# A hybrid decoder layer on one core: full 128-row low parts of the keys in the attention scores

## The chip, the cores and the metric

The kernel runs on one core of one Trainium2 chip. The time is device microseconds of an execution, given as the median of several runs. A profile is one more execution, taken by the hardware profiler; its span reaches from the first to the last instruction. TensorE (PE) multiplies, with its weight loads shown apart (PEld); VectorE (DVE), ScalarE (ACT) and GpSimd (POOL) do the elementwise work; SyncE (SP) issues the DMAs.

## What is computed

One decoder layer for 512 tokens of width 1024 in fp32: a token mixer of three groups (sparse attention, gMLP, a Conformer convolution), cross-attention into 256 memory tokens, and a gated ConvFFN. The change lies in the sparse attention. It has 8 heads of width 64 in 2 key/value groups; with 512 tokens, all 8 blocks of the selected branch are taken and the window covers everything, so both branches are causal softmax attention, each with its own keys and values, beside a compressed branch:

```python
s_s = jnp.einsum("bgrtd,bgtmd->bgrtm", qb, gk).astype(jnp.float32) * scale
p_s = masked_softmax(s_s, mask_s)
o_s = jnp.einsum("bgrtm,bgtmd->bgrtd", p_s.astype(gv.dtype), gv)
...
s_w = jnp.einsum("bgrtd,bgkd->bgrtk", qb, kw).astype(jnp.float32) * scale
p_w = masked_softmax(s_w, mask_w)
o_w = jnp.einsum("bgrtk,bgkd->bgrtd", p_w.astype(vw.dtype), vw)
...
o = (gates[..., 0:1] * unblock(o_c) + gates[..., 1:2] * unblock(o_s)
     + gates[..., 2:3] * unblock(o_w))
```

## The kernel before

Every factor of a product is split into a high part that TensorE's faster fp32 form holds exactly and a low rest, so that a product takes three matmuls (high x high, high x low, low x high).

**Keys and queries.** Tokens lie along the free dimension, head dimensions along the 128 rows. `ev_q` (line 566) makes one 128-row tile per head, with the high part of the query in the 64 rows of its group g and the low part in the other 64. `ev_k` (line 584) makes for each branch b: for each group a tile `kh_[b, g]` with the high part of the keys in both halves, and one tile `kl_[b]` with the low parts, group 0 in rows 0 to 63 and group 1 in rows 64 to 127. All of these tiles are slabs, 56 buffers of 128 x 512 that are used in turn.

**Scores.** `scores()` (line 985) goes through 16 units (token block i of 128, group g, branch b), four heads in each, and W = 128 (i + 1) keys. A head takes a pair of matmuls into one bank, with the query tile as the weights. The first contracts all 128 rows and so gives (high + low query) x high key; the second contracts the 64 rows of the group and gives high query x low key:

```python
E.matmul(o3[:, jj, :], q, kh_[b, g][:, :W], start=True, stop=False)
E.matmul(o3[:, jj, :], q[hs], kl_[b][hs, :W], start=False, stop=True)
```

Four heads of 128 keys, two of 256, or one of 384 or 512 go into one bank (tag "s", two banks).

**What follows a score.** `soft` (line 1006): VectorE adds the mask and takes the row extreme, ScalarE takes the exponential with its sum, VectorE the reciprocal, GpSimd scales by reciprocal and gate (tiles "tpr"). `turns` and `mix`: TensorE transposes the probabilities, ScalarE and VectorE split them into high ("tB") and low ("tC"), and TensorE multiplies both with the values into one bank. Work on the compressed branch ("tcd", "tcph", "tcpl"), on the memory's keys and values (weights "whi" and "wlo", split by ScalarE and, for the memory, GpSimd), the gMLP and the convolution is mixed in.

**What sets the order.** Each engine executes its instructions in the order in which the program issues them. From line 452 on, that order is made while the program is built: `Lanes` (line 44) holds many generators, books an assumed cost for every instruction (line 65) and lets that step go next which can start first by these costs, by priority among near equals. A matmul's cost there goes by its columns. All instructions are issued through line 186, so the rows of the trace are told apart by their tiles.

Of the kernel before, what the change touches and what calls it, by code (L numbers as in the profile page):

```python
# [9 lines left out]
F32 = mybir.dt.float32  # L10
# [31 lines left out]


class Lanes:
    """Puts the steps of concurrent generators in order: each generator yields the engine of its next step, what the
    step reads and the kinds of slots it opens; the step that can start first goes next, and among those of one
    engine that are about as early, the most urgent one."""

    LAT = {"E": 0.18, "S": 0.14, "V": 0.12, "G": 0.14, "D": 0.0}
    OWN = {"E": 0.0, "S": 0.05, "V": 0.12, "G": 0.05, "D": 0.0}  # L50
# [139 lines left out]
def body(ctx, tc, xT, memT, memN, cmask, cmaskT, w_a, w_v, w_u, w_c1, gains, smalls, ws_t, bcs, w_o, w_q, w_k, w_vm,  # L190
# [3 lines left out]
    ln = Lanes(PB)  # L194
    V, S, G, E, Q = [Engine(ln, k, e) for k, e in zip("VSGED", (nc.vector, nc.scalar, nc.gpsimd, nc.tensor, nc.sync))]
# [11 lines left out]
    def nm(s):  # L207
        uid[0] += 1
        return f"{s}_{uid[0]}"

    def slab(shape=(P, T), dt=F32R):
        return psl.tile(list(shape), dt, name=nm("sl"), tag="slab", bufs=NSLAB)

    def tmp(tag, shape=(P, T), dt=F32):
        return ln.open(tag, pt.tile(list(shape), dt, name=nm("t" + tag), tag=tag, bufs=TB[tag]))

    def tiny(shape, dt=F32):
        return pt.tile(list(shape), dt, name=nm("ty"), tag="tiny", bufs=24)
# [4 lines left out]
    def col(n):  # L223
        return pt.tile([P, n], F32, name=nm("rc"), tag="rcol", bufs=4)

    def ps(tag):
        return ln.open(tag, pp.tile([P, T], F32, name=nm("ps"), tag="bank", bufs=8))
# [12 lines left out]
    def mm3(o, ah, al, bh, bl, start, stop):  # L240
        E.matmul(o, ah, bh, start=start, stop=False)
        E.matmul(o, ah, bl, start=False, stop=False)
        E.matmul(o, al, bh, start=False, stop=stop)
# [10 lines left out]
        for _ in gen:  # L254
            pass

    # weight stream
    specs = [(("a", m), w_a[m], (8, 128)) for m in range(12)]
    specs += [(("c1", i), w_c1[i], (16, 64)) for i in range(2)]
    specs += [(("v", c), w_v[:, k0:k1, :], (k1 - k0, 280)) for c, (k0, k1) in enumerate(((0, 3), (3, 6), (6, 8)))]  # L260
# [9 lines left out]
    order = {s[0]: n for n, s in enumerate(specs)}  # L270
# [32 lines left out]
    def ahead(key, n=2):  # L303
        prep(order[key] + n)

    # constants
    gn = pc.tile([P, NGAIN], F32, name="gn")
    sm = pc.tile([P, NSMALL], F32, name="sm")
    cm = pc.tile([P, T], F32, name="cm")
# [1 line left out]
    def gv(name):  # L311
        a, b = GAIN[name]
        return gn[:, a:b]
# [55 lines left out]
            mm3(o[:, :width], wh[:, k, :], wl[:, k, :], hi, lo, first and n == 0, last and n == len(ks) - 1)  # L369
            yield  # L370

    # start: first norm and the first two column tiles side by side
    n1 = Norm("g_mix")
    x = [slab(dt=F32) for _ in range(KD)]
    # wake the activation table and the tensor engine's clock while the first loads run
    wz = tmp("A")
    V.memset(wz, 0.0)
    S.activation(tiny([P, 4]), wz[:, 0:4], AF.Copy)
# [70 lines left out]
    wsr = slab(dt=F32)  # L449
    load(wsr, ws_t)  # L450

    # from here on lanes
    for tag, n in list(PB.items()) + list(TB.items()) + [("raw", NRAW), ("whi", NW), ("wlo", NW), ("bank", 8)]:
        ln.slots[tag] = [0.0] * n
    for o, tag in zip(zc, ("mm", "mm", "s", "s")):
# [14 lines left out]
    def pr(kind, j=0):  # L470
        return prio[kind][j]
# [32 lines left out]
    def spent(key):  # L504
        ln.done(*ready.pop(key))

    # depthwise convolution
    cw = pc.tile([P, 62], F32, name="cwh")
    V.tensor_scalar(cw, sv("cw"), 0.5, None, op0=ALU.mult)
    conv_acc = [slab(dt=F32) for _ in range(2)]  # L510
# [28 lines left out]
                                   op0=ALU.mult, op1=ALU.add)  # L539
        ln.mark(("taps", c), acc)  # L540

    # projection tiles
    qs, kh_, kl_ = {}, {}, {}

    def ev_cmp(kv, o):
# [38 lines left out]
    def ev_k(b, o):  # L584
        yield "V", [o], ["A"]
        kf = tmp("A")
        V.tensor_mul(kf, o, r_bc)
        ln.done(o)
        kl_[b] = slab()
        for g in range(2):  # L590
            kh_[b, g] = slab()
            hs = slice(64 * g, 64 * g + 64)
            for half in (g, 1 - g):
                yield "S", [kf], []
                S.activation(kh_[b, g][64 * half:64 * half + 64], kf[hs], AF.Copy)
            yield "V", [kh_[b, g]], []
            V.tensor_sub(kl_[b][hs], kf[hs], kh_[b, g][hs].bitcast(F32))
        ln.done(kf)
        ln.mark(("k", b), kl_[b], kh_[b, 0], kh_[b, 1])

    vs, gate, gz = [None] * NT, [None] * NT, [slab([P, 2, 256], F32) for _ in range(NT)]

# [82 lines left out]
                ln.add(pr("ev", 4), ev_u(hf, i, o))  # L685
        ln.mark("projected")

    # compressed blocks: second layer and scores of all tokens
    w2 = pc.tile([64, 2, 192], F32R, name="w2s")
    split(w2[:, 0, :], w2[:, 1, :], sv("w2")[0:64, :])  # L690
    vcz, kcz, sct = [], [], []
# [64 lines left out]
        for i in range(NT):  # L756
            ln.add(pr("cmp", i), compressed(i))

    # memory: statistics and parts, then keys and values as filler
    rm_col = col(2)  # L760
    rm_bc = pt.tile([P, MEM], F32, name="rm_bc", tag="rmbc", bufs=1)
    g_m = gv("g_m")
# [86 lines left out]
                ln.add(pr("memev", 1), mem_ev("mv", 2 * c + mt, o))  # L849
        ln.mark("quiet")  # L850

    # token-major tails of the gMLP and convolution groups
    g_out = gv("g_out")
    y_hi, y_lo = [None] * KD, [None] * KD
    gx = []
# [121 lines left out]
        yield from put_back(y, 6, i)  # L977
        ln.done(y)

    # native sparse attention  # L980
    units = [(i, g, b) for i in range(NT) for g in range(2) for b in range(2)]
    probs, left = {}, {}
    cmp_p, yts = {}, {}
# [1 line left out]
    def scores():  # L985
        yield "E", ["attend"], []
        for u in units:
            i, g, b = u
            W = P * (i + 1)
            hp = {0: 4, 1: 2, 2: 1, 3: 1}[i]  # L990
            hs = slice(64 * g, 64 * g + 64)
            isl = slice(i * P, (i + 1) * P)
            probs[u], left[u] = [None] * 4, 4
            mn, sm_ = tiny([P, 4]), tiny([P, 4])
            for n in range(4 // hp):
                yield "E", [("q", 4 * g + n * hp + jj) for jj in range(hp)] + [("k", b)], ["s", "pr"], pr("score", i)
                o = ps("s")
                p_ = tmp("pr")
                o3 = o[:, :hp * W].rearrange("p (h w) -> p h w", h=hp)
                for jj in range(hp):  # L1000
                    q = qs[4 * g + n * hp + jj][:, isl]
                    E.matmul(o3[:, jj, :], q, kh_[b, g][:, :W], start=True, stop=False)
                    E.matmul(o3[:, jj, :], q[hs], kl_[b][hs, :W], start=False, stop=True)
                ln.add(pr("soft", i), soft(u, n * hp, hp, o, p_, mn, sm_))

    def soft(u, j0, hp, o, p_, mn, sm_):
        i, g, b = u
        W = P * (i + 1)
        o3 = o[:, :hp * W].rearrange("p (h w) -> p h w", h=hp)
        p3 = p_[:, :hp * W].rearrange("p (h w) -> p h w", h=hp)  # L1010
        for jj in range(hp):
            yield "V", [o], []
            V.tensor_tensor_reduce(out=p3[:, jj, :], in0=o3[:, jj, :], in1=cm[:, T - W:], scale=1.0, scalar=3e38,
                                   op0=ALU.add, op1=ALU.min, accum_out=mn[:, j0 + jj:j0 + jj + 1])
        ln.done(o)
        for jj in range(hp):
            yield "S", [p_], []
            S.activation(p3[:, jj, :], p3[:, jj, :], AF.Exp, scale=-1.0, bias=mn[:, j0 + jj:j0 + jj + 1],
                         accum_out=sm_[:, j0 + jj:j0 + jj + 1])
        yield "V", [p_, ("v", i)], []  # L1020
        f = tiny([P, hp])
        V.reciprocal(f, sm_[:, j0:j0 + hp])
        for jj in range(hp):
            yield "G", [f, p_], []
            G.tensor_scalar(p3[:, jj, :], p3[:, jj, :], f[:, jj:jj + 1],
                            gate[i][:, 4 * g + j0 + jj, 1 + b:2 + b], op0=ALU.mult, op1=ALU.mult)
            probs[u][j0 + jj] = p3[:, jj, :]
        left[u] -= hp
        if left[u] == 0:
            ln.mark(("p", u), *probs[u])  # L1030
# [140 lines left out]
                                   y_hi[kt][:, isl].bitcast(F32), op0=ALU.mult, op1=ALU.subtract)  # L1171
        ln.mark(("yn", i), *y_lo[:4])

    # projections of the residual stream
    def tiles(name, parts, deps, after, phases):
        """The first two tiles side by side, phase by phase of their sums, then one tile after the other."""
        o, count = {}, KD if name != "up" else 2
        jobs = [(m, k) for ks in phases for m in range(2) for k in ks]
        jobs += [(m, k) for m in range(2, count) for ks in phases for k in ks]
        first, last = phases[0][0], phases[-1][-1]  # L1180
        for m, k in jobs:
            key = (name, m)
            yield "E", [("w",) + key] + deps(k), ["mm"] if k == first else []
            if k == first:
                o[m] = ps("mm")
            wh, wl = ready[key]
            mm3(o[m], wh[:, k, :], wl[:, k, :], parts[0][k], parts[1][k], k == first, k == last)
            if k == last:
                spent(key)
                ln.add(pr("resid", ("o", "q", "ox", "up").index(name)), after(m, o[m]))  # L1190
# [39 lines left out]
        ln.done(o)  # L1230
        yield from pow_rstd(out_t, tot, 1.0 / D)

    # cross-attention
    n2, n3 = Norm("g_x"), Norm("g_f")
    rx, sc_col = col(NT), col(NT)
    xs, kp, vp = {}, {}, {}
# [108 lines left out]
        oh[k], ol[k] = hi, lo  # L1345
        ln.mark(("oh", k), hi, lo)

    # gated convolutional FFN
    rf = col(NT)
    rf_bc = pt.tile([P, T], F32, name="rf_bc", tag="rbc", bufs=1)  # L1350
    pending = []
# [12 lines left out]
        return iter(())  # L1364

    class Pairs:
        """The parts of a norm's tiles as two lists."""
        def __init__(self, norm, j):
            self.norm, self.j = norm, j

# [6 lines left out]
    for g in range(2):  # L1377
        zz = tmp("A")
        V.memset(zz, 0.0)
        kcz.append((slab(), slab()))  # L1380
        for t_ in kcz[g]:
            V.tensor_copy(t_, zz)
        ln.done(zz)
    first_w = order["a", 5]
    ln.add(pr("load"), stream(first_w, order["up", 4]))
    ln.add(pr("ev", 7), conv_group(0))
# [13 lines left out]
    lists = lambda norm: (Pairs(norm, 0), Pairs(norm, 1))  # L1400
# [12 lines left out]
    x = xs8  # L1413
    st_ = {}

    # gated convolutional FFN
    fw, fb = sv("fw"), sv("fb")
    ah, al = [], []
    st_["late"] = []
# [45 lines left out]
            split(ah[-1], al[-1], tv)  # L1465
            yield

    # down projection and final norm
    gfin = gv("g_fin")
    acc4 = pt.tile([P, T], F32, name="acc4", tag="acc", bufs=1)  # L1470

# [35 lines left out]
    for m in range(KD):  # L1507
        cuts = (slice(0, T),) if m < KD - 1 else (slice(0, 256), slice(256, T))
        ws_ = []
        for ci, cs in enumerate(cuts):  # L1510
# [4 lines left out]
            for c in range(3):  # L1515
# [3 lines left out]
                for kk in range(8 if c < 2 else 6):  # L1519
                    k = 8 * c + kk  # L1520
# [114 lines left out]
```

## Time and profile before

| | |
|---|---|
| median of 3 runs (lowest, highest) | 808.39 us (804.48, 810.5) |
| span of the profiled execution | 801.6 us, 10865 instructions |
| busy TensorE / its weight loads | 785.8 us (98%) / 657.1 us (82%) |
| busy VectorE / ScalarE / GpSimd | 532.5 / 393.8 / 128.0 us |

The scores run from 97 to 240 us. Matmuls are pipelined and the ends of their rows are modelled, so the rows are best read by their starts: the distance from one start to the next is what an instruction takes of TensorE. A row of a weight load names the matmul's tiles, and its form says how many rows it loads (128*128 or 64*128).

### The profile page before, as it was taken

What the parts mean: (1) busy time and instruction counts of PE and PEld (TensorE: products, weight loads), DVE (VectorE), ACT (ScalarE), POOL (GpSimd) and SP (SyncE); (2) the same over time, 40 slices, a digit from 0 to 9 for tenths busy, and PEclk for the clock granted to TensorE, in tenths of its full rate; (3) what the DMA queues carried; (4) which work ended last, traced back from release to release, by engine and by line L of the source; (5) the groups of instructions that cost most, each with busy time, mean ns of one, the idle gap of its engine ahead of it and who ended that gap; (6) DMA issues with size and microseconds to landing.
All of it is one profiled execution on the core that took longest, in us unless ns stands there. A gap on an engine that the chain in (4) does not pass through costs nothing.

```text
span 801.6 us, 10865 instructions
## 1 busy us (share of the span) xinstructions
PE 785.8 (98%) x4024; PEld 657.1 (82%) x4024; DVE 532.5 (66%) x1014; ACT 393.8 (49%) x787; POOL 128.0 (16%) x182
## 2 busy tenths in 40 slices
PE   8999999999999999999999999999999999999995
PEld 6888988878778888888888888888888888888884
DVE  7799857979878865555564787777766767332333
ACT  7455657586677753545442554444443344232221
POOL 0000046647978200100000000000000000000002
PEclk9999989989999999999999999999999999999998
DMA  8522500210222532211032323222222222433303
GB/s 277 183 100 86 182 1 26 82 53 28 105 84 102 202 113 105 79 53 53 32 127 79 105 105 105 82 103 106 86 98 105 91 87 72 125 92 99 99 20 105
DMA packets 26644, 76.96 MB, mean 96 GB/s; under 512 B 2912, under 2 KB 7008, under 8 KB 26592
## 3 DMA queue, kind: packets, MB, share of 16 engines
q1 hardware_dynamic: 26048, 75.76, 27.7%
q8 instruction: 31, 0.51, 0.3%
q10 hardware_dynamic: 544, 0.52, 0.2%
q14 instruction: 21, 0.17, 0.1%
HBM read 74.17 MB, written 2.10 MB: 95 GB/s over the span
## 4 chain that ended last, share of the span: by engine, by line
PE 90%; POOL 4%; DVE 2%; ACT 2%; issue 1%; SPq 1%; DMA 1%; DVEq 0%; POOLq 0%
PE ps L186 90%; POOL wlo L186 2%; POOL ty L186 1%; SPq L186 1%; DMA sl<-in_xT 1%; POOL tpr L186 1%; ACT sl L186 0%; DVE tpr L186 0%; DVE sl L186 0%; ACT whi L186 0%; ACT tpr L186 0%; DVE wlo L186 0%; ACT tD L186 0%; DVE ty L186 0%; DVE tA L186 0%
## 5 line engine op out<-in xcount | busy, mean ns | idle before, releaser
L186 PE MATMUL ps<-sl,whi 128*128 128x512 f32 (+1 forms) x1804 | 531.9, 378 | 0.9 <-DVE sl L186 0.6
L186 PEld LDWEIGHTS ps<-sl,whi 128*128 128x128 f32 x1804 | 331.2, 189 | 64.2 <-DVE sl L186 1.1
L186 PE MATMUL ps<-sl,wlo 128*128 128x512 f32 (+1 forms) x902 | 340.0, 377 | 0.5 <-DVE wlo L186 0.5
L186 ACT ACTIVATE whi<-raw 128x512 fp32r<-128x512 f32 (+4 forms) x227 | 147.4, 673 | 172.6 <-PE ps L186 143.8
L186 PEld LDWEIGHTS ps<-sl,wlo 128*128 128x128 f32 x902 | 170.0, 188 | 31.9 <-DVE wlo L186 0.9
L186 DVE TENSOR_TENSOR wlo<-raw,whi 128x512 fp32r<-128x512 f32 (+5 forms) x163 | 141.2, 878 | 75.9 <-ACT whi L186 69.3
L186 POOL TENSOR_TENSOR ty<-ty,nhalf 128x1 f32<-128x1 f32 (+1 forms) x22 | 13.4, 616 | 365.7 <-DVE ty L186 365.7
L186 DVE TENSOR_TENSOR sl<-ps,sl 128x512 f32<-128x512 f32 (+3 forms) x45 | 29.6, 659 | 61.3 <-PE ps L186 47.9
L186 PE MATMUL ps<-whi,sl 128*128 128x256 f32 (+1 forms) x320 | 65.7, 295 | 0.0
L186 PE MATMUL ps<-sl,sl 128*128 128x256 f32 (+3 forms) x252 | 63.8, 355 | 0.6 <-DVE sl L186 0.6
L186 POOL TENSOR_TENSOR wlo<-raw,whi 128x256 fp32r<-128x256 f32 x64 | 55.5, 889 | 12.6 <-ACT whi L186 12.6
L186 DVE TENSOR_TENSOR tA<-ps,rf_bc 128x512 f32<-128x512 f32 x44 | 30.3, 688 | 40.7 <-PE ps L186 40.7
L186 PEld LDWEIGHTS ps<-sl,sl 128*128 128x128 f32 x252 | 41.5, 193 | 17.3 <-issue 9.4
L186 PEld LDWEIGHTS ps<-whi,sl 128*128 128x128 f32 x320 | 52.7, 194 | 1.6 <-issue 0.5
L186 POOL TENSOR_SCALAR tpr<-tpr,ty,gate 128x128 f32<-128x128 f32 (+3 forms) x64 | 43.5, 688 | 25.7 <-DVE ty L186 14.6
L186 DVE SCALAR_TENSOR_TENSOR sl<-sl,cwh,sl 128x511 f32<-128x511 f32 (+29 forms) x60 | 47.0, 812 | 0.2
L186 PE MATMUL ps<-wlo,sl 128*128 128x256 f32 (+1 forms) x160 | 46.1, 288 | 0.0
L186 ACT ACTIVATE tpr<-tpr,ty 128x128 f32<-128x128 f32 (+3 forms) x64 | 35.4, 554 | 6.9 <-DVE ty L186 6.8
L186 ACT ACTIVATE tB<-ps 128x512 fp32r<-128x512 f32 x48 | 27.8, 593 | 20.6 <-PE ps L186 20.4
L186 DVE CUSTOM_DVE_ANT_0 tpr<-ps,cm 128x128 f32<-128x128 f32 (+3 forms) x64 | 29.6, 480 | 11.6 <-PE ps L186 11.6
L186 DVE TENSOR_TENSOR tC<-ps,tB 128x512 fp32r<-128x512 f32 x48 | 32.0, 681 | 7.6 <-ACT tB L186 7.6
L186 ACT ACTIVATE tD<-sl 128x512 f32<-128x512 f32 (+1 forms) x33 | 19.0, 583 | 34.3 <-DVE sl L186 33.0
(141 smaller groups left out, 729.5 us busy)
## 6 DMA issues: line engine op xcount, KB each, us to landing
raw<-in_w_up SPq DMA_DIRECT2D x44, 512.0 KB, 3.2
raw<-in_w_dn SPq DMA_DIRECT2D x16, 512.0 KB, 3.5
raw<-in_w_a SPq DMA_DIRECT2D x10, 512.0 KB, 3.9
sl<-in_xT SPq DMA_DIRECT2D x16, 256.0 KB, 4.6
raw<-in_w_k SPq DMA_DIRECT2D x8, 512.0 KB, 3.2
raw<-in_w_vm SPq DMA_DIRECT2D x8, 512.0 KB, 3.7
raw<-in_w_o SPq DMA_DIRECT2D x8, 512.0 KB, 3.2
raw<-in_w_q SPq DMA_DIRECT2D x8, 512.0 KB, 3.2
```

What stands on the lines that cost most here:

```text
L186: return fn(*a, **k)
```

## The change

Each branch and group gets a low tile of its own, `kl_[b, g]`, with the low parts in the 64 rows of its group and zeros in the other 64. The four tiles are allocated ahead of the scheduled part, and GpSimd fills their other halves with zeros. The second matmul of a pair takes the whole query tile and the whole low tile. The low half of the query meets the zeros, so the sum is the same. Comments and docstrings are dropped as well, which moves the line numbers only.

```diff
@@ -586,7 +586,6 @@
         kf = tmp("A")
         V.tensor_mul(kf, o, r_bc)
         ln.done(o)
-        kl_[b] = slab()
         for g in range(2):
             kh_[b, g] = slab()
             hs = slice(64 * g, 64 * g + 64)
@@ -594,9 +593,9 @@
                 yield "S", [kf], []
                 S.activation(kh_[b, g][64 * half:64 * half + 64], kf[hs], AF.Copy)
             yield "V", [kh_[b, g]], []
-            V.tensor_sub(kl_[b][hs], kf[hs], kh_[b, g][hs].bitcast(F32))
+            V.tensor_sub(kl_[b, g][hs], kf[hs], kh_[b, g][hs].bitcast(F32))
         ln.done(kf)
-        ln.mark(("k", b), kl_[b], kh_[b, 0], kh_[b, 1])
+        ln.mark(("k", b), kl_[b, 0], kl_[b, 1], kh_[b, 0], kh_[b, 1])
...
             W = P * (i + 1)
             hp = {0: 4, 1: 2, 2: 1, 3: 1}[i]
-            hs = slice(64 * g, 64 * g + 64)
             isl = slice(i * P, (i + 1) * P)
...
                     q = qs[4 * g + n * hp + jj][:, isl]
                     E.matmul(o3[:, jj, :], q, kh_[b, g][:, :W], start=True, stop=False)
-                    E.matmul(o3[:, jj, :], q[hs], kl_[b][hs, :W], start=False, stop=True)
+                    E.matmul(o3[:, jj, :], q, kl_[b, g][:, :W], start=False, stop=True)
...
+    for b in range(2):
+        for g in range(2):
+            kl_[b, g] = slab()
+            rest = slice(64 * (1 - g), 64 * (1 - g) + 64)
+            G.memset(kl_[b, g][rest].bitcast(F32), 0.0)
     first_w = order["a", 5]
```

On TensorE, VectorE, ScalarE and SyncE the program has the same instructions in the same order before and after; only the operands of the low matmuls differ. GpSimd's order gains four instructions. This is its start before, with the first norm's reciprocal root ("rc", 128x4) and the first work of the compressed branch behind it:

```order
L186 ISA
L186 TENSOR_TENSOR rc_289<-ty_290,nhalf 128x4
L186 TENSOR_TENSOR tcd_1153<-tcd_1153,ty_1198 128x256
L186 TENSOR_TENSOR rc_352<-ty_1236,nhalf 128x2
L186 TENSOR_SCALAR tpr_1119<-tpr_1119,ty_1228,gate_1022 128x128 x4
```

And the same place with the change:

```order
L186 ISA
L186 TENSOR_TENSOR rc_289<-ty_290,nhalf 128x4
L186 MEMSET sl_372 64x512
L186 MEMSET sl_374 64x512
L186 MEMSET sl_376 64x512
L186 MEMSET sl_378 64x512
L186 TENSOR_TENSOR tcd_1159<-tcd_1159,ty_1204 128x256
L186 TENSOR_TENSOR rc_352<-ty_1242,nhalf 128x2
L186 TENSOR_SCALAR tpr_1125<-tpr_1125,ty_1234,gate_1028 128x128 x4
```

The four fills stand behind the reciprocal root and ahead of all that GpSimd does for the attention; the rest of its order is as before.

## Rows read from the trace of the kernel before

**Rows 1.** The page's first part: busy time, share of the span and instructions.

```profile
PE 785.8 (98%) x4024; PEld 657.1 (82%) x4024; DVE 532.5 (66%) x1014; ACT 393.8 (49%) x787; POOL 128.0 (16%) x182
```

**Rows 2.** Busy us by stage: stretch, engines with instructions, PE clock, DMA share, GB/s.

```profile
97.00:132.00 35.00, 35.00 (x187) 28.06 (x185) 20.63 (x99) 21.59 (x80) 16.08 (x31) 0.90 0.09 32
132.00:170.00 38.00, 37.07 (x245) 30.88 (x244) 35.08 (x84) 27.75 (x65) 22.30 (x27) 1.00 0.24 77
170.00:187.00 17.00, 16.98 (x80) 12.78 (x81) 12.36 (x37) 12.81 (x36) 6.21 (x10) 0.81 0.06 17
187.00:213.00 26.00, 24.98 (x179) 21.91 (x177) 25.32 (x62) 15.06 (x44) 25.45 (x30) 1.00 0.23 78
213.00:240.00 27.00, 27.00 (x162) 20.96 (x161) 21.28 (x55) 18.86 (x49) 22.17 (x29) 1.00 0.24 82
```

**Rows 3.** Weight loads in order of time: start, us, form [idle before <-what ended it].

```profile
152.28 0.19 PEld L186 LDWEIGHTS ps<-sl,sl 128*128 128x128 f32 x1
152.65 0.18 PEld L186 LDWEIGHTS ps<-sl,sl 64*128 64x128 f32 x1 [0.18 <-issue]
153.01 0.19 PEld L186 LDWEIGHTS ps<-sl,sl 128*128 128x128 f32 x1 [0.18 <-DVE sl L186]
...
153.75 0.19 PEld L186 LDWEIGHTS ps<-tB,sl 128*128 128x128 f32 x1 [0.18 <-ACT tB L186]
153.86 0.19 PEld L186 LDWEIGHTS ps<-tC,sl 128*128 128x128 f32 x1
154.09 0.59 PEld L186 LDWEIGHTS ps<-sm,tpr 128*128 128x128 f32 x4
154.65 0.19 PEld L186 LDWEIGHTS ps<-tcph,sl 128*128 128x128 f32 x1
```

**Rows 4.** 64-row score loads of five stages: count | busy us, mean ns | idle before.

```profile
L186 PEld LDWEIGHTS ps<-sl,sl 64*128 64x128 f32 x32 | 6.3, 196 | 3.5 <-issue 0.2
...
L186 PEld LDWEIGHTS ps<-sl,sl 64*128 64x128 f32 x12 | 2.2, 183 | 2.2 <-issue 2.0
...
L186 PEld LDWEIGHTS ps<-sl,sl 64*128 64x128 f32 x6 | 1.2, 200 | 1.8 <-issue 1.8
...
L186 PEld LDWEIGHTS ps<-sl,sl 64*128 64x128 f32 x5 | 0.9, 183 | 1.2 <-issue 1.2
...
L186 PEld LDWEIGHTS ps<-sl,sl 64*128 64x128 f32 x10 | 1.8, 183 | 2.4 <-issue 2.4
```

**Rows 5.** Weight loads in order of time around scores of 128 and 256 columns.

```profile
108.29 1.99 PEld L186 LDWEIGHTS ps<-sl,sl 128*128 128x128 f32 x8
110.35 0.19 PEld L186 LDWEIGHTS ps<-whi,sl 128*128 128x128 f32 x1
110.46 0.19 PEld L186 LDWEIGHTS ps<-wlo,sl 128*128 128x128 f32 x1
...
112.21 1.13 PEld L186 LDWEIGHTS ps<-sl,sl 128*128 128x128 f32 x4
113.47 0.19 PEld L186 LDWEIGHTS ps<-sm,rc 128*128 128x128 f32 x2
```

**Rows 6.** Weight loads around one pair of 512 columns.

```profile
204.28 0.19 PEld L186 LDWEIGHTS ps<-sl,sl 128*128 128x128 f32 x1
...
205.14 0.19 PEld L186 LDWEIGHTS ps<-tB,sl 128*128 128x128 f32 x1 [0.24 <-issue]
```

**Rows 7.** Busy us in three stretches around the falls of the clock.

```profile
101.50:108.20 6.70, 6.70 (x25) 5.68 (x25) 4.13 (x26) 3.72 (x17) 2.67 (x6) 0.50 0.00 0
165.50:169.70 4.20, 3.53 (x15) 1.83 (x13) 3.78 (x14) 4.15 (x10) 1.46 (x3) 1.00 0.26 62
169.80:176.50 6.70, 6.47 (x22) 5.09 (x23) 4.56 (x16) 4.13 (x12) 3.78 (x6) 0.50 0.01 2
```

**Rows 8.** VectorE's waits in 97 to 132: us in total, times, longest.

```profile
DVE tpr L186 <- PE ps L186: 8.4, 7, 3.8
```

**Rows 9.** GpSimd in order of time: its first work for the attention [idle before].

```profile
105.42 0.62 POOL L186 TENSOR_TENSOR tcd<-tcd,ty 128x256 f32<-128x256 f32 x1 [79.19 <-DVE ty L186]
```

## Prediction

> **What bounds the kernel now.** The page's first part comes first: TensorE is busy for 98% of the span [rows 1]. That is a number about coverage and not about useful work, because a matmul that starts late is still counted until its modelled end. So the second view is the busy time by stage, cut where the attention scores run [rows 2]. From 97 to 240 us, TensorE is covered almost throughout in every stage. Next to it stands a different engine each time: VectorE with 35.08 of 38 us in 132 to 170, and GpSimd with 25.45 of 26 us in 187 to 213. Those two stages are tight on two engines at once; 97 to 132, 170 to 187 and 213 to 240 are tight on TensorE alone.
>
> The third view is the order in time of the weight loads [rows 3]. This is where the change bites. Elsewhere the load of the next weights starts together with the matmul before it, so that loads follow each other at the pace of the columns: the 512 columns of tB and tC stand 0.23 us apart (153.86 to 154.09), and of the four 128-column transposes that follow, the first is loaded during tC, so that the other three take 154.65 - 154.09 - 0.23 = 0.33 us, 0.11 us each. Around a score pair it is otherwise. The load of the 64-row part at 152.65 and the load of the next 128-row matmul at 153.01 each stand about 0.37 us after the load before them, and the row itself gives 0.18 us of idleness put down to "issue" or, at 153.01, to an old semaphore: the load had no data to wait for. Both directions cost it, 128 to 64 rows and back. All such 64-row loads of the stage are in rows 4.
>
> **The change, part by part.**
>
> *Score pairs.* There are 16 units of four heads, so 64 pairs (a full-height matmul and a low one), 16 pairs for each width of 128, 256, 384 and 512 columns. The price of a pair before is the distance of loads over a run of pairs; the price after is two matmuls at the pace of the other 128-row matmuls.
> - 128 columns: eight matmuls from 108.29 to 110.35 [rows 5], 2.06 / 4 = 0.515 us a pair; after 2 x 0.11 = 0.22. Saved: 0.295.
> - 256 columns: 112.21 to 113.47 for two pairs, 0.63 a pair; a 256-column matmul stands at 110.46 - 110.35 = 0.11 [rows 5], after 0.22. Saved: 0.41.
> - 384 columns: 152.28 to 153.75 for two pairs, 0.735 a pair [rows 3]. No 128-row matmul of 384 columns stands free of such a neighbour, so its price lies between 0.11 (256) and 0.23 (512); I take the middle, 0.17, after 0.34. Saved: 0.395, with bounds 0.275 and 0.515.
> - 512 columns: 204.28 to 205.14, 0.86 a pair [rows 6]; after 0.46. Saved: 0.40.
>
> Sum on TensorE: 16 x (0.295 + 0.41 + 0.395 + 0.40) = 16 x 1.50 = 24.0 us, with the bounds at 384 columns 22.1 to 25.9. The low matmul streams as many columns as before, so 128 rows instead of 64 add nothing that these rows show; the distance of 128-row loads is the price used.
>
> *Clock.* In 101.5 to 108.2 us the granted clock was 0.50, which is 1.2 instead of 2.4 GHz [rows 7]. Ahead of it TensorE ran 128-column score pairs at 0.5 us each. With pairs at 0.22 us that stretch becomes as dense as the transposes of rows 3, which ran at full clock. If the fall goes away, the 6.7 us shrink by at most half, 3.3 us; if it stays, by nothing. I take 2. The second fall, 169.8 to 176.5, has a different forerunner: in 165.5 to 169.7 TensorE was busy for only 3.53 of 4.2 us and VectorE for 3.78. That is a wait for other engines, which the change does not remove, so I let it stand: 0, with 3.3 as the far bound.
>
> *What arrives at the end, by stage* [rows 2, 4]. An earlier score is worth something only as far as softmax, probability scaling and the transposed copies follow. Each stage gets the smaller of TensorE's saving and what the tightest helper can give back.
> - 97 to 132: 32 pairs, 16 x 0.295 + 16 x 0.41 = 11.3, with the clock 13.3. VectorE is idle 35 - 20.63 = 14.4 us there, and the largest piece of that, 8.4 us, ends when scores arrive [rows 8]. It can follow nearly all of it; I take 12.
> - 132 to 170: 12 pairs, 4.8 us on TensorE, but VectorE has only 38 - 35.08 = 2.9 us of idleness. I take 2.
> - 170 to 187: 6 pairs, 2.4 us. VectorE has 4.6 us idle, ScalarE 4.2. I take 2.
> - 187 to 213: 5 pairs, 2.0 us on TensorE, but GpSimd has 26 - 25.45 = 0.55 us idle. It splits the memory weights and scales the probabilities in a fixed order, so it can start this run earlier, but not do it faster. I take 0.5.
> - 213 to 240: 10 pairs, 4.0 us; GpSimd has 4.8 idle, VectorE 5.7. I take 2.
>
> Sum 12 + 2 + 2 + 0.5 + 2 = 18.5; 0.5 of it I leave to new short waits: **18 us**. After 240 there are no score pairs, and TensorE carries the rest, so an early start is kept.
>
> *Zero rows.* GpSimd gets four fills of 64 rows by 512 columns, right after the reciprocal root of the first norm. The nearest row is its product of 128 x 256 in 0.62 us; twice the columns give at most 1.24 us each, 5.0 in all, and below that nothing. Its next work starts at 105.42 after 79.19 us of idleness [rows 9]: this gap hides them, and the scores read them from 97 on, 65 us later. If the cover were gone, 5 us would stand in front of the compressed branch. Two more of the 56 large buffers are taken; no instruction on any engine changes its place by it.
>
> *Against the median.* The sum stands against the profiled execution, whose span is 801.6 us; the median of the runs is 808.39, so 6.8 us lie around the span or between runs. The span should come to about 783.6 and the median to 808.4 - 18 = **790.4 us**.
>
> **A rule against it.** The 64-row matmuls occupy half the array, so the kernel before could be getting overlap that the change throws away. What the trace shows is none: the 64-row load at 152.65 starts 0.37 us behind the full-height one, more than the 0.23 us of a whole 512-column matmul, and the next full-height load comes as late again [rows 3]. If overlap existed, full height would cost half of each low matmul's streaming, 16 x (0.055 + 0.055 + 0.085 + 0.115) = 5.0 us, and the time would be 813. The Trainium skill, TensorEngine Tiling (Array Packing), section Key Properties, says that tiles work independently, so that different ones can load and multiply in parallel, and offers up to twice the speed for a contraction of 64. By that rule, the trace disagrees here, since each 64-row matmul stands alone between two that need all rows.
>
> **Rivals.**
> - *All of it arrives.* VectorE and GpSimd were late only because TensorE was, and both falls of the clock or one of them vanish: 24.0 + 3.3 = 27.3, at 781 us. For it: 8.4 us of VectorE's idleness end at scores. Against it: 0.55 us of slack on GpSimd in 187 to 213.
> - *Little arrives.* The loop from score to scaled probability sets the pace already in 97 to 132; VectorE gives back only its longest single wait for scores there, 3.8 us [rows 8], and half of the other 4.6, some 6 us, and 1 in each later stage but GpSimd's: 6 + 3 = 9, at 799 us, down to 4 us and 804 if it is the longest wait alone. Against it: VectorE is idle for two fifths of that stage.
> - *The pause is not from the row count*, but from two sums into one bank in a row; then nothing changes: 808. Against it: tB and tC also add into one bank, at 0.23 us.
> - *Slower.* A TensorE that runs ahead waits more, and waits like those of 165.5 to 169.7 are followed by 6.7 us at half clock, 3.3 us each where TensorE sets the end. Six new falls eat the 18 us (6 x 3.3 = 19.8); from eight on (26.4 - 18 = 8.4) the kernel is slower by over 1%, near 817. Against it: only one such fall stands in 143 us now, and where GpSimd is the bound the lower clock is free.
>
> **How the numbers follow.** Forecast, 12 to 22 us gained: 0.56. All of it: 0.18. Little: 0.16. No effect: 0.05. Slower by waits 0.04, by lost overlap 0.01. About 1%, 8 us, is what a measurement can tell here. Faster by more than that: the first two and half of "little", 0.82. Within 1%: 0.14. Slower: 0.04. The range runs from all of it, 781, to the near end of "little", 800; about 0.8 lies in it. The forecast's own range is 786 to 796.
>
> **What would show it.** Right: no idle time in front of loads around the scores, 384-column matmuls near 0.17 us apart, full clock from 97 to 132, and in 187 to 213 a GpSimd as full as before with TensorE now waiting for it. Wrong: loads still 0.37 us apart (no effect), VectorE waiting for scores as long as before (little), or more stretches at 0.50 in 97 to 240 (slower).

## The result and the profile after

The changed kernel takes 783.74 us (median; 782.99 to 784.88) against 808.63 us (804.48 to 810.5) for the kernel before. The ratio is 0.9719 with a 95% interval of 0.968 to 0.9757, so it is faster by 2.4 to 3.2%. A second set on another chip gave 783.1 against 806.09 us, 0.9722 (0.9681 to 0.9763). The forecast was 790.4 us in 781 to 800: direction and range hold, but the middle was 6.7 us too slow, and 783.74 lies outside the narrower 786 to 796 that the prediction calls the forecast's own range. The span of the profiled execution is 782.3 us, against 783.6 forecast.

First the busy time by stage of the changed kernel, in the columns of [rows 2] (stretch, TensorE, weight loads, VectorE, ScalarE, GpSimd, TensorE clock, DMA share, GB/s):

```profile
97.00:132.00 35.00, 34.99 (x286) 34.04 (x285) 31.90 (x124) 29.53 (x104) 24.90 (x41) 1.00 0.17 57
132.00:170.00 38.00, 35.31 (x241) 30.80 (x240) 36.28 (x100) 33.32 (x81) 20.51 (x25) 1.00 0.21 68
170.00:187.00 17.00, 17.00 (x134) 16.37 (x133) 16.43 (x40) 10.07 (x32) 17.00 (x22) 1.00 0.28 91
187.00:213.00 26.00, 23.16 (x150) 20.45 (x149) 21.53 (x52) 16.27 (x43) 22.97 (x27) 0.93 0.26 83
213.00:240.00 27.00, 25.71 (x190) 23.59 (x189) 23.33 (x77) 21.36 (x64) 23.10 (x34) 1.00 0.29 92
```

In 97 to 132 us TensorE starts 286 matmuls instead of 187, the clock is 1.00 instead of 0.90, and VectorE goes from 20.63 to 31.90 us of work in the same 35. GpSimd's full stretch (25 us without idle time, by slices of 5 us) moves from 190 to 215 us before to 170 to 195 us, and TensorE has idle time in 132 to 170 and 187 to 240.

Next, weight loads of the changed kernel in order of time, at scores of 128, 256, 384 and 512 columns (start, us, form):

```profile
102.56 0.98 PEld L186 LDWEIGHTS ps<-sl,sl 128*128 128x128 f32 x8
103.46 0.19 PEld L186 LDWEIGHTS ps<-whi,sl 128*128 128x128 f32 x1
...
107.56 0.54 PEld L186 LDWEIGHTS ps<-sl,sl 128*128 128x128 f32 x4
108.03 0.19 PEld L186 LDWEIGHTS ps<-whi,sl 128*128 128x128 f32 x1
...
144.97 0.65 PEld L186 LDWEIGHTS ps<-sl,sl 128*128 128x128 f32 x4
145.60 0.19 PEld L186 LDWEIGHTS ps<-tB,sl 128*128 128x128 f32 x1
145.79 0.19 PEld L186 LDWEIGHTS ps<-tC,sl 128*128 128x128 f32 x1
...
186.40 0.76 PEld L186 LDWEIGHTS ps<-sl,sl 128*128 128x128 f32 x4
187.21 0.19 PEld L186 LDWEIGHTS ps<-tB,sl 128*128 128x128 f32 x1
187.44 0.19 PEld L186 LDWEIGHTS ps<-tC,sl 128*128 128x128 f32 x1
```

These answer to [rows 3, 5, 6]. Eight loads of 128 columns take 103.46 - 102.56 = 0.90 us (2.06 before), four of 256 take 0.47 (1.26). At 384 and 512 columns one more step is needed. A load starts together with the matmul before it, and the first score load there follows a 128-column transpose; so the first 0.11 us belong to that transpose, and the load of tC starts when the last score matmul has made way for that of tB. Four matmuls of 384 columns thus take 145.79 - 144.97 - 0.11 = 0.71 us (1.47 before), four of 512 take 187.44 - 186.40 - 0.11 = 0.93 (2 x 0.86 before). Per pair that is 0.225, 0.235, 0.355 and 0.465 us, where the working had 0.22, 0.22, 0.34 and 0.46. No idle time stands in front of these loads. The saving at 384 columns, 0.735 - 0.355 = 0.38, lies inside the bounds given.

TensorE executes the same 4024 matmuls in the same order in both kernels. So the lead can be read matmul by matmul: the start before less the start after, of the one that opens each stage of the trace before. The last column is the forecast by stage.

| stage of the kernel before | lead at its end | gained in it | forecast |
|---|---|---|---|
| to 97 us | -0.4 | | |
| 97 to 132 | 12.5 | 12.9 | 12 |
| 132 to 170 | 13.7 | 1.2 | 2 |
| 170 to 187 | 18.5 | 4.8 | 2 |
| 187 to 213 | 17.7 | -0.8 | 0.5 |
| 213 to 240 | 19.9 | 2.2 | 2 |
| 240 to 275 | 19.2 | -0.7 | |

The forecast took off another 0.5 us for short waits without naming a stage. From 275 us to the end the lead stays at 19.2 us. GpSimd's zero fills run at 26.7 us, in the gap that [rows 9] show (count | busy us, mean ns | idle before):

```profile
L186 POOL MEMSET sl<- 64x512 f32 x4 | 2.1, 519 | 0.2
```

### The profile page after: what moved, and what is told of

Read it like the earlier page. It is cut to its first block, busy times and chain, and to the rows that moved or that the text cites. A ratio compares the mean times of both kernels' runs of the same rounds, so it can differ in the third digit from the quotient of the medians.

```text
span 782.3 us, 10870 instructions
## 1 busy us (share of the span) xinstructions
PE 762.9 (98%) x4024; PEld 650.3 (83%) x4024; DVE 531.4 (68%) x1014; ACT 392.9 (50%) x787; POOL 130.7 (17%) x186
## 4 chain that ended last, share of the span: by engine, by line
PE 87%; POOL 5%; DVE 2%; ACT 2%; DMA 2%; issue 1%; SPq 0%; DVEq 0%; POOLq 0%
PE ps L186 87%; POOL wlo L186 3%; DMA sl<-in_xT 1%; POOL ty L186 1%; POOL tpr L186 1%; DVE sl L186 1%; DMA tpr<-in_memT 0%; SPq L186 0%; ACT tpr L186 0%; ACT whi L186 0%; ACT tD L186 0%; ACT sl L186 0%; DVE tpr L186 0%; DVE ty L186 0%; DVE wlo L186 0%
## 5 line engine op out<-in xcount | busy, mean ns | idle before, releaser
L186 PE MATMUL ps<-whi,sl 128*128 128x256 f32 (+1 forms) x320 | 63.6, 288 | 0.0
L186 PE MATMUL ps<-sl,sl 128*128 128x256 f32 (+3 forms) x252 | 46.4, 321 | 1.1 <-DVE sl L186 1.1
L186 PEld LDWEIGHTS ps<-sl,sl 128*128 128x128 f32 x252 | 36.0, 193 | 3.6 <-DVE sl L186 1.4
L186 DVE SCALAR_TENSOR_TENSOR tC<-tA,sm,tC 128x511 f32<-128x511 f32 (+1 forms) x44 | 32.9, 748 | 3.8 <-ACT tC L186 3.0
L186 ACT ACTIVATE tB<-tB 128x512 f32<-128x512 f32 x22 | 13.9, 633 | 41.4 <-DVE tB L186 41.4
```

What stands on the lines that cost most here:

```text
L186: return fn(*a, **k)
```

## Experiments

### The row count, or the separate tiles?

```diff
+hs = slice(64 * g, 64 * g + 64)
...
-E.matmul(o3[:, jj, :], q, kl_[b, g][:, :W], start=False, stop=True)
+E.matmul(o3[:, jj, :], q[hs], kl_[b, g][hs, :W], start=False, stop=True)
```

> The changed kernel with one thing undone: the four separate low tiles and their zero fills stay, but the low matmul again contracts the 64 rows of its group. If the row count alone makes the gain, this is as slow as the kernel before: 806 to 810 us, and the 64-row weight loads again stand 0.2 us late on either side. If the gain came from the separate tiles (fewer waits on a tile shared by two groups), it keeps it: 784 to 790 us. The fills themselves cost nothing measurable (GpSimd stands idle for 79 us there).

Measured: 805.73 us against 806.37, ratio 0.9999 (0.9963 to 1.0035). The weight loads stand apart again, as in [rows 3]:

```profile
153.48 0.18 PEld L186 LDWEIGHTS ps<-sl,sl 64*128 64x128 f32 x1 [0.18 <-issue]
153.84 0.19 PEld L186 LDWEIGHTS ps<-tB,sl 128*128 128x128 f32 x1 [0.18 <-issue]
153.95 0.19 PEld L186 LDWEIGHTS ps<-tC,sl 128*128 128x128 f32 x1
```

The separate tiles and their fills give and cost nothing that stands out of the interval of 0.4% on either side. The gain hangs on the 128 rows.

### A 64-row matmul, or the change to and from it?

The kernel before, with the matmuls of a bank put in another order; only the first of a bank now starts a sum and only the last ends it:

```diff
 for jj in range(hp):
     q = qs[4 * g + n * hp + jj][:, isl]
-    E.matmul(o3[:, jj, :], q, kh_[b, g][:, :W], start=True, stop=False)
-    E.matmul(o3[:, jj, :], q[hs], kl_[b][hs, :W], start=False, stop=True)
+    E.matmul(o3[:, jj, :], q, kh_[b, g][:, :W], start=jj == 0, stop=False)
+for jj in range(hp):
+    q = qs[4 * g + n * hp + jj][:, isl]
+    E.matmul(o3[:, jj, :], q[hs], kl_[b][hs, :W], start=False, stop=jj == hp - 1)
```

> The kernel before, all low matmuls still on 64 rows, but in each bank of scores the full-height matmuls of its heads come first and the low ones behind them, so that a bank of four heads (128 columns) has 2 changes of row count instead of 8, one of two heads (256) 2 instead of 4, and those of 384 and 512 columns have 2 as before. Theory change: the price is on the change between row counts, about 0.2 us each (0.15 at 128 columns), so 4 banks save 6 x 0.15 and 8 banks 2 x 0.2: 0.9 x 4 + 0.4 x 8 = 6.8 us on TensorE before 132 us, of which 4 to 6 arrive: 801 to 805 us, and low matmuls in a row follow each other at 0.11 us. Rival row count: a 64-row matmul is slow by itself; then nothing is gained, 807 to 810 us, and low matmuls in a row stand 0.25 us apart.

Measured: 793.41 us, ratio 0.9845 (0.978 to 0.9909). Its weight loads at 128 columns (four heads) and 256 columns (two heads):

```profile
99.53 1.12 PEld L186 LDWEIGHTS ps<-sl,sl 128*128 128x128 f32 x8
100.72 0.20 PEld L186 LDWEIGHTS ps<-sm,sl 128*128 128x128 f32 x2
...
106.93 0.73 PEld L186 LDWEIGHTS ps<-sl,sl 128*128 128x128 f32 x4
107.80 0.19 PEld L186 LDWEIGHTS ps<-sm,rc 128*128 128x128 f32 x2
```

Eight matmuls of 128 columns, four of them on 64 rows, take 1.19 us with two changes of row count. That is 2.06 with eight changes and 0.90 with none, so (2.06 - 0.90) / 8 = 0.145 us a change, and 0.145 for each of the two that are left. At 256 columns it is 0.87 with two changes, 1.26 with four and 0.47 with none: 0.2 us a change. So the price is on the change, and a 64-row matmul among its like costs no more than a full one. TensorE's saving is 4 x 0.87 + 8 x 0.39 = 6.6 us, as expected. The time fell by 13 us, to well below the 801 to 805 us expected. The clock goes with the rest: the profile of this kernel has no fall near 101 us, as the next section shows.

### Why do the runs say 23 to 25 us where the traces say 19?

> The kernel before, once more, to see its runs' spans and granted clocks beside each other. The changed kernel ended 24.9 us earlier by the medians, but its profiled execution only 19.3 us earlier by the spans (801.6 to 782.3). Theory 1: the profiled execution of before was a quick one; its runs differ in how many stretches ran at the lower clock, and an average run has 4 to 6 us more of them than the profile on which the prediction was built. Then time falls as the mean clock rises over these runs, the slowest near clock 0.975 and the quickest at 0.987 or above. Theory 2: the difference lies outside the span (launch and end); then the spans of all runs lie near 801 to 803 us and the clocks near 0.987. Median 805 to 809 us either way.

Measured: 806.79 us over 10 runs, ratio 1.0003 (0.9968 to 1.0037). Theory 1 holds. The runs lie 1.93 us above their spans (median), so what is around the span is small and constant; the spans themselves go from 800.1 us at a mean clock of 0.989 to 809.4 at 0.979, and those of the 19 runs beside it from 800.7 us at 0.989 to 809.4 at 0.976. The profile of this copy (span 805.0 us) shows where, in the columns of [rows 7]:

```profile
101.00:121.50 20.50, 20.50 (x73) 17.03 (x73) 7.86 (x46) 8.28 (x39) 5.55 (x12) 0.50 0.00 1
```

The clock falls at the same place as in [rows 7], where the scores of 128 columns begin, but stays low for 20.5 us and not for 6.7. Read matmul by matmul, the copy falls 5.4 us behind the first profile between 101.5 and 132 us. It makes up 2.5 us from 170 to 176.5 us, where it has no second fall, and ends 3.4 us later. The profile on which the prediction rests had a short first fall. Where the falls of the other runs lie is not on record; only their mean clocks are.

The fall at 101 us goes with the expensive pairs. The four profiles of kernels whose early low matmuls have 64 rows, each between full ones, all have it, for 6.7, 13.7 and twice 20.5 us. With the low matmuls grouped and in the changed kernel the same stretch reads:

```profile
101.50:121.50 20.00, 20.00 (x146) 17.90 (x146) 15.37 (x82) 17.50 (x72) 13.63 (x28) 1.00 0.01 1
...
101.00:121.50 20.50, 20.50 (x168) 19.75 (x168) 18.27 (x91) 19.58 (x78) 17.12 (x33) 1.00 0.01 1
```

Why the fall lasts for different times in different executions stays open.

### Which stage carries the gain?

Two kernels, each with full rows for half of the token blocks. This is the edit for blocks 0 and 1; its counterpart has `i >= 2`:

```diff
+hs = slice(64 * g, 64 * g + 64)
...
-E.matmul(o3[:, jj, :], q, kl_[b, g][:, :W], start=False, stop=True)
+if i < 2:
+    E.matmul(o3[:, jj, :], q, kl_[b, g][:, :W], start=False, stop=True)
+else:
+    E.matmul(o3[:, jj, :], q[hs], kl_[b, g][hs, :W], start=False, stop=True)
```

> Full rows for the low matmuls of token blocks 0 and 1 alone (128 and 256 columns, 32 pairs, all in 97 to 132 us); blocks 2 and 3 contract 64 rows as before. By the prediction's table this stage gives 12 us and the later ones nothing: 795 to 798 us (against a median of 808.6). If the later stages, bound by VectorE and GpSimd, give part of it back, 800 to 804 us. If the gain at the end comes from the later stages, 806 to 809 us.

> The counterpart of the run on blocks 0 and 1: full rows for the low matmuls of token blocks 2 and 3 alone (384 and 512 columns, 32 pairs, all behind 132 us); blocks 0 and 1 contract 64 rows as before. On TensorE these pairs cost 32 x 0.4 = 12.7 us less. By the prediction's table the later stages let 6.5 us through: 799 to 802 us against a median near 806.4, and the fall of the clock near 101 us stays, as in the kernel before. If later stages are elastic (VectorE and GpSimd were only waiting for TensorE), nearly all arrives: 793 to 796 us. If they are full, 804 to 807 us. Together with the gain of blocks 0 and 1 (15.8 us) it should make up the 22.7 to 24.9 us of the whole change.

Measured: blocks 0 and 1 alone 790.58 us (788.8 to 792.93), ratio 0.9812 (0.9758 to 0.9865), 15.8 us quicker. Blocks 2 and 3 alone 801.37 us (796.36 to 806.29), ratio 0.9935 (0.9899 to 0.997), 4.1 us quicker. The first is over 4 us better than the 795 to 798 us expected. In the trace its lead is 12.4 us at 132 and still 12.4 at 500, as the table above has it for that stage. What comes on top goes with the fall at 101 us: its profile has none, and the mean clocks of its runs are 0.990 to 0.995. The second kernel keeps the fall, and its runs spread over 10 us:

```profile
101.00:121.50 20.50, 20.50 (x74) 17.08 (x74) 8.07 (x47) 8.27 (x38) 5.32 (x11) 0.50 0.00 1
```

So the 32 early pairs are worth four times the 32 late ones, although TensorE saves more on the late ones (16 x (0.38 + 0.395) = 12.4 us against 16 x (0.29 + 0.395) = 11.0). Part of this is the clock at 101 us, which changed with the early pairs alone. 15.8 + 4.1 is 3 to 5 us short of the whole change. The profile of the second kernel shows two more falls of the clock, of 6.8 us at 176 and 3.4 us at 217, which the changed kernel has not or has only once; whether they explain the difference in its other runs was not tried.

### What holds back the rest?

VectorE relieved (most of the convolution is left out), GpSimd relieved (the low parts of the memory weights are replaced by a scaled copy of the high ones), and both; the planner books the costs of the full instructions, so that every engine's order stays:

```diff
-V.scalar_tensor_tensor(acc[:, j:], hp[:, :T - j], cw[:, c * 31 + 30 - j:c * 31 + 31 - j], acc[:, j:],
-                       op0=ALU.mult, op1=ALU.add)
+cj = cw[:, c * 31 + 30 - j:c * 31 + 31 - j]
+ln.account("V", "scalar_tensor_tensor", (acc[:, j:], hp[:, :T - j], cj, acc[:, j:]), {})
+nc.vector.scalar_tensor_tensor(acc[:, j:j + P], hp[:, :P], cj, acc[:, j:j + P], op0=ALU.mult, op1=ALU.add)
...
-(G if mem_w else V).tensor_sub(lo[:, cs], raw[:, cs], hi[:, cs].bitcast(F32))
+if mem_w:
+    ln.account("G", "tensor_sub", (lo[:, cs], raw[:, cs], hi[:, cs].bitcast(F32)), {})
+    nc.gpsimd.tensor_scalar(lo[:, cs], hi[:, cs].bitcast(F32), nhalf[:, 0:1], nhalf[:, 1:2],
+                            op0=ALU.mult, op1=ALU.mult)
+else:
+    V.tensor_sub(lo[:, cs], raw[:, cs], hi[:, cs].bitcast(F32))
```

> The changed kernel with VectorE relieved: each of the 60 tap additions of the depthwise convolution works on 128 columns instead of up to 511 (most of the convolution is left out), about 0.55 us less each, 35 of them in the attention stages, 19 us of VectorE's time there; every engine's order stays. Theory: VectorE bounds 132 to 170 us, so the 2.6 us for which TensorE waits there for VectorE go, and the hidden part too: 2 to 5 us quicker, 779 to 782 us (783.7 with the full taps). Rival: VectorE is only busy, not in the way: 783 to 784.5 us. GpSimd's full stretch stays as long as it was and only starts earlier.

> The changed kernel with GpSimd relieved: for the memory weights it writes a scaled copy of the high part (one input, by rows of the same width near 0.48 us) in place of the difference (two inputs, 0.89 us), so the low parts of these weights are not computed; 64 instructions, about 26 us of GpSimd's time; every engine's order stays. Theory: GpSimd bounds the changed kernel in 170 to 195 and 216 to 241 us, where TensorE waits 2.8 us for it and once falls to half clock behind such waits: 3 to 6 us quicker, 778 to 781 us, and no wait of TensorE for these weights. Rival: it only fills its time: 783 to 784.5 us.

> Both reliefs at once: short taps on VectorE and the scaled copy on GpSimd (most of the convolution and the low parts of the memory weights are left out); orders as before. If the two bounds are what keeps TensorE's 24 us and its clock from arriving in full, this is the sum of the two single reliefs or more: 774 to 779 us, with TensorE waiting less than 1 us in 97 to 240. If a third limit stands behind them (the loop from score to scaled probability), it is no quicker than the better single one.

Measured: short taps 778.36 us (777.54 to 780.49), scaled copy 778.02 (776.8 to 779.0), both 777.01 (775.54 to 777.6); 5.4, 5.7 and 6.7 us quicker than the changed kernel. Both single reliefs land in the ranges of their theories. But the two do not add up (5.4 + 5.7 = 11.1), and both together are only 1.0 us quicker than the better one, so for the most part they lift the same limit, or a third one stands behind both; the runs do not tell these apart. Nor did short taps work as expected. These are TensorE's waits in 97 to 240 us with them (us in total, times, longest):

```profile
PE ps L186 <- DVE sl L186: 1.5, 2, 1.2
PE ps L186 <- DVE tY L186: 1.3, 2, 1.1
PE ps L186 <- DVE ty L186: 0.2, 1, 0.2
```

In the changed kernel they are 3.9 us for VectorE and 2.8 for GpSimd. So short taps take away the waits for GpSimd, and most of the waits for VectorE stay; that VectorE's own time is in the way is not shown. With both reliefs TensorE still waits 2.6 us, where less than 1 was expected. In the trace with both, the lead over the kernel before is 27.8 us at the end, 8.6 more than in the changed kernel; the prediction's rival "all of it arrives" stood at 27.3.

The link between the two is seen in the changed kernel, GpSimd above, VectorE below, in order of time:

```profile
134.84 5.56 POOL L186 TENSOR_TENSOR wlo<-raw,whi 128x256 fp32r<-128x256 f32 x3 [4.47 <-ACT whi L186]
```

```profile
132.76 5.21 DVE L186 SCALAR_TENSOR_TENSOR sl<-sl,cwh,sl 128x501 f32<-128x501 f32 x8
```

Three subtractions on GpSimd take 5.56 us, the first of them 3.73 us while VectorE runs taps back to back. The taps are not slowed here: they follow each other every 5.21 / 8 = 0.65 us, so GpSimd alone waits. All of these subtractions in 97 to 241 us (duration ns min/median/max), first in the changed kernel, then with short taps:

```profile
L186 POOL TENSOR_TENSOR wlo<-raw,whi x61: 719/744/3735, 122.5 to 238.7; 128x256 fp32r<-128x256 f32 x61
```

```profile
L186 POOL TENSOR_TENSOR wlo<-raw,whi x64: 718/739/1000, 120.5 to 240.8; 128x256 fp32r<-128x256 f32 x64
```

The median does not move; the long ones go. In other places it works the other way too. Taps on VectorE in the changed kernel, first at 60 to 93 us with GpSimd idle, then at 97 to 200 us:

```profile
L186 DVE SCALAR_TENSOR_TENSOR sl<-sl,cwh,sl x21: 722/734/747, 59.4 to 91.8; 128x508 f32<-128x508 f32 x2, 128x507 f32<-128x507 f32 x2, 128x506 f32<-128x506 f32 x2, 128x511 f32<-128x511 f32 x1
...
L186 DVE SCALAR_TENSOR_TENSOR sl<-sl,cwh,sl x30: 710/760/1219, 100.1 to 193.1; 128x492 f32<-128x492 f32 x2, 128x491 f32<-128x491 f32 x2, 128x490 f32<-128x490 f32 x2, 128x489 f32<-128x489 f32 x2
```

VectorE's subtractions with one input in PSUM are not slowed, in 97 to 241 us:

```profile
L186 DVE TENSOR_TENSOR tC<-ps,tB x39: 664/681/693, 111.8 to 235.5; 128x512 fp32r<-128x512 f32 x39
```

So short taps relieve GpSimd without touching it. The Trainium skill, GPSIMD Engine Reference, section Key points, says that GpSimd shares its SBUF interfaces with VectorE and contends with VectorE instructions of two SBUF inputs; a tap is one, and the trace agrees (up to 1.22 us against 0.73, and no change for the subtractions from PSUM). The scaled copy, expected at 0.48 us, took 0.70 us in the mean beside full taps and 0.60 beside short ones, so that it took about 64 x (0.89 - 0.70) = 12 us off GpSimd beside full taps, and not 26.

### A version that beats both?

Part of GpSimd's scaling moved to ScalarE: every second head of token block 3, all heads of it, and every second head of blocks 2 and 3. The changed kernel ran beside them.

```diff
+if i == 3 and (j0 + jj) % 2 == 1:
+    fg = tiny([P, 1])
+    V.tensor_tensor(out=fg, in0=f[:, jj:jj + 1], in1=gate[i][:, 4 * g + j0 + jj, 1 + b:2 + b], op=ALU.mult)
+    yield "S", [fg, p_], []
+    S.activation(p3[:, jj, :], p3[:, jj, :], AF.Copy, scale=fg)
+    probs[u][j0 + jj] = p3[:, jj, :]
+    continue
```

> The changed kernel once more, on the same chip as the three variants beside it. 782 to 786 us, with a spread of 2 to 3 us over its runs against 8 to 9 us of the kernel before, since the long fall of the clock near 101 us is gone.

> The changed kernel with some of GpSimd's scaling moved: in token block 3 every second head's probabilities are scaled by ScalarE (reciprocal times gate made on VectorE, one column), so 8 instructions of 0.94 us leave GpSimd, about 7.5 us, and 8 of some 0.6 us go to ScalarE, which has 8 to 13 us idle in 165 to 200 us. The order is made anew by the planner. If GpSimd and its contention with VectorE bound 170 to 241 us, 2 to 4 us quicker than the changed kernel: 779 to 782 us. If the new order or ScalarE's load takes it back, 783 to 786 us.

> As the variant beside it, but all 16 scalings of token block 3 go to ScalarE: 15 us off GpSimd, some 10 us onto ScalarE, which is then as busy as GpSimd was. If the relief of GpSimd counts most, 778 to 781 us; if ScalarE becomes the bound (it also makes the high parts that every split waits for), 783 to 788 us.

> As the first variant, with every second head of token blocks 2 and 3 on ScalarE: 16 scalings, 8 x 0.94 + 8 x 0.72 = 13 us off GpSimd. The blocks of 384 columns run in 132 to 187 us, where GpSimd has idle time and ScalarE 4 to 5 us; so no more than the first variant, 779 to 783 us, and if ScalarE's earlier load delays the softmax there, 784 to 787 us.

Measured: the changed kernel 783.1 us (782.65 to 783.67), the variants 795.17, 795.54 and 794.0. The changed kernel's runs lie within 1.0 us, those of the kernel before beside them within 6.8 (802.56 to 809.33). All three variants are 7 us or more slower than the slowest that was expected of them. GpSimd is relieved, with 16.09 us of work in 213 to 240 instead of 23.10, but the planner makes another order of it. In the first variant TensorE waits more behind the scores, and the clock falls for long:

```profile
245.00:254.00 9.00, 6.26 (x48) 5.44 (x47) 8.26 (x34) 6.78 (x24) 3.44 (x7) 1.00 0.71 253
...
254.30:268.00 13.70, 10.67 (x24) 6.93 (x25) 9.97 (x28) 7.04 (x21) 1.39 (x3) 0.50 0.39 132
```

The moved work and the new order were not told apart. No kernel here that computes the whole layer beats the changed one.

## Why the prediction was right, and where it was off

**The cause and its price.** Right. The pauses belong to the change of row count; with 128 rows everywhere they are gone, and the prices after are 0.225 to 0.465 us a pair, each within 0.015 of the one worked out. The sum at these prices is 16 x (0.29 + 0.395 + 0.38 + 0.395) = 23.4 us, against 24.0 and inside 22.1 to 25.9. A small error: the stages of the working hold 33 late pairs, not 32, because a load on the border of two stretches is counted in both.

**What the stages let through.** The total is close, 19.2 us in the traces where the working had 18, but partly by luck: 2.5 of the 19.2 us are the second fall of the clock, of the next paragraph, which only the first profile of the kernel before had. Without it 16.7 stand against 18. VectorE did follow in 97 to 132 us: its waits for scores fell from 8.4 us [rows 8] to one of 0.6, and its work there rose to 31.90 us. The stage 132 to 170 gave 1.2 us where 2 were forecast, but that VectorE's taps hold it back is not shown. With VectorE and GpSimd relieved it gives 2.2 of the some 4.6 us that TensorE saves there. In the changed kernel the chain of work that ended last goes there through a load of the memory's tokens, and not through the taps (start, us):

```profile
142.37 3.70 DMA tpr<-in_memT
146.09 0.52 ACT sl L186
146.63 0.69 DVE sl L186
```

GpSimd's stretch was passed on earlier without becoming shorter; TensorE now waits for it, as the prediction asked for (us in total, times, longest, in 187 to 213):

```profile
PE ps L186 <- POOL wlo L186: 1.6, 3, 0.8
PE ps L186 <- POOL tpr L186: 1.2, 1, 1.2
```

**Clock, second fall.** Wrong: it was left standing at 170 us, and it is gone, which makes 170 to 187 us 4.8 us better instead of 2. The copy of the kernel before has no fall there either (clock 1.00 from 169.7 to 183.5 us, where the same matmuls lie), and gains 2.5 us by it with the same program. So this fall comes and goes, the runs do not show that the change removed it, and the change itself is left with 4.8 - 2.5 = 2.3 us in this stage, near the 2 forecast. In the changed kernel's profile a new one of 3.4 us stands behind the waits just shown, as the rival "slower" described it, with one instance instead of six; its second profiled execution has none in the scores:

```profile
188.50:194.90 6.40, 3.56 (x25) 2.71 (x24) 6.40 (x17) 3.63 (x10) 6.40 (x8) 1.00 0.20 56
...
194.90:198.30 3.40, 3.40 (x11) 2.71 (x12) 2.02 (x7) 1.79 (x4) 3.40 (x5) 0.51 0.20 64
```

**Against the median.** This is the step that failed. It set the 18 us off against the median as if the 6.8 us between the profiled span and the median were fixed. What is fixed is 2.0 us. The other 4.8 lie inside the spans and go with the clock: over 29 later runs of the kernel before the mean clocks are 0.991 to 0.976, and the changed kernel's are 0.991 to 0.996. That most of it is the fall at 101 us is argued from the profiles above, where its length is what differs most; the changed kernel has no such fall. The working gave the clock at 101 us at most 3.3 us, by the one length that its profile showed; an average run had more to give. Some 2 of the 4.8 us are also the small sample: 808.39 is the median of three runs, and later sets of 7 to 19 runs have 805.5 to 806.8. The error of 6.7 us is these 4.8, the 1.2 by which the lead in the traces was larger than 18 (less than what the second fall gave), and 0.7 by which the changed kernel's profiled execution (784.44 us) lies above its median.

**The rule against it.** The trace's answer held: full rows made the pairs cheaper at every width, so there was no overlap to lose. The factor of two that the prediction gives with Key Properties stands on the same page of the Trainium skill, TensorEngine Tiling (Array Packing), in section Theoretical Speedup. Two such tiles at once would be matmuls on different halves of the rows. Wherever a kernel here uses 64 rows, the low matmuls of a bank are on the same half, so no run shows it.

**Rivals.** The measured median is nearer to "all of it arrives" (781 us) than to the forecast, but not for its reason: in the traces a lead of 19.2 us arrives, of the 27.3 of this rival, and it came near 27.3 only with VectorE and GpSimd both relieved. "Little arrives", "the pause is not from the row count" and "slower" are refuted by the runs above.

## What to carry to other kernels

Look at the distance between weight loads, not at busy TensorE: a matmul that contracts half of the rows between full ones cost some 0.15 to 0.2 us at each change here, and zero rows, or putting such matmuls side by side, buy that back. A gain on the busiest engine arrives stage by stage, as far as the work that follows on other engines can keep up. And compare the profiled span with the other runs before building on it: a spread of 1% between runs is itself something that a change can remove.

## What was not expected of the hardware

At one and the same place of the program the granted clock stayed at 0.50 for 6.7 us in one execution and for 20.5 us in another of the same kernel; the spans of its runs lie up to 9 us apart, the longer the lower their mean clock. And VectorE and GpSimd slow each other strongly in places: a tap of 0.73 us took up to 1.22 us, and one subtraction of 0.74 us took 3.7 us, while the taps beside it went on at their usual pace.
